# An attention stage with four rooms for probability parts and two for exponentials, and W_out's low parts and the first mixed heads on VectorE

## The chip, the cores and the metric

One core of a Trainium2 chip runs the whole kernel. The time is the device time of one execution in microseconds (us), here always the median of several executions. The engines of the core are named as the profile names them: PE (TensorE, matrix products; PEld its weight loads), DVE (VectorE), ACT (ScalarE), POOL (GpSimd) and SP (SyncE, whose queue issues nearly all transfers; SPq are its issues). They run side by side, each in its own order, and wait for one another through semaphores.

## The reference

One layer of an encoder for 2048 tokens of width 1024. Three groups of heads read the same normalised projection, are gated, and are projected back:

```python
proj = h @ w_in[l]
aq, ak, av, bqkv, ba, bb, mq, z = jnp.split(proj, pts, axis=-1)
...
    def block(qblk):
        sc = jnp.einsum('bkgqd,bksd->bkgqs', qblk, kt).astype(jnp.float32)
        p = jax.nn.softmax(sc, axis=-1).astype(vt.dtype)
        return jnp.einsum('bkgqs,bksd->bkgqd', p, vt)
...
mix = jnp.concatenate([y_a, y_b, y_m], axis=-1) * jax.nn.silu(z)
x = x + rms_norm(mix @ w_out[l], norm_post_w[l])
```

`y_a` is softmax attention with 8 heads over all 2048 tokens, `y_b` a gated delta rule, and `y_m` attention of 4 heads into 256 memory tokens. The change lies in the stage that computes `y_a` and `y_m`, in the preparation of `w_out`, and in the first rows of `mix` that are made ready for `mix @ w_out`.

## The kernel before

Products that need float32 accuracy are made of float16 parts: a value is a high part (its float16 cast) plus a low part (what the cast left over), and a product is three matmuls (high by high, high by low, low by high).

The stages follow each other: projections and the delta rule up to about 1300 us, attention from 1307 to about 2085 us, then the output projection. Attention is cut into 136 blocks: 64 units of 256 queries of one head, two blocks of 128 queries (`qb` 0 and 1) each, and after every fourth of the first 32 units one memory unit, which is one block. So there are 72 units; their index `n` is that of `prefetch`.

A block goes through these steps, one pass of the main loop apart (`lag(1)`, `lag(2)`, up to `LAG` = 5):

- pass i: `score(k)` for k = 0 and 1: six matmuls of 128x512 into a PSUM pair (`sa`; three such pairs exist), and `top(k)`: a maximum over 1024 scores on DVE; after k = 1 two short DVE instructions give the softmax offset (`mx`).
- pass i+1: `expo(k)` on ACT: the exponentials of 1024 scores into a float32 tile `P` (tag `P`), which frees the PSUM pair; then `high` on ACT: `P` is cast into the high half of a float16 tile `hl` (tag `hl`).
- pass i+2, k = 0: `low`: P minus its high part into the low half of `hl`, 768 keys on DVE and the other 1280 (with one of overlap, which keeps the two in order) on POOL; then SP issues a transposing transfer of the whole `hl`, 1 MB, to `PT`.
- from pass i+6: `value`: PE multiplies `PT` with V (`pva`), in slots between the score matmuls.

A `P` room is needed from a block's first exponential to the end of POOL's `low`; an `hl` room from `high` until the transposing transfer has landed. Both tiles take 8 KB in each partition. Before the change there are three rooms of each.

PE, ACT and DVE run in the order in which the code is written in this stage (they are pinned). POOL and SP are not: a scheduler places their instructions, and then they too run in that fixed order.

`prefetch(n)` prepares the output projection during the last 32 units (n from 40): for odd n up to 55 `split_wo` splits one 128x1024 piece of W_out into its parts (`wo`), fetched one unit before into the only `wraw` room (`wor`); for n = 57, 59 and 61 `split_mix` gates, scales and splits the first four heads of `mix` for one block of 128 tokens (`mer` times `mr_r`, into `me`), fetched for even n. It runs at the head of a pass, with `qb` = 0, ahead of the exponentials. With POOL as the engine `split_wo` takes two ACT instructions and one on POOL; `split_mix` one on ACT and three on POOL.

At the end of attention the remaining heads of `mix` for the first two token blocks (`mr`, `mg`) borrow rooms of the tags `P` and `hl`, and PE fills the gaps with output matmuls on the three early `me` blocks (`fillers`).

Of the kernel before, what the change touches and what calls it, by code (L numbers as in the profile page):

```python
# [22 lines left out]
S = 2048  # L23
# [14 lines left out]
def hybrid_layer(ctx: ExitStack, tc: tile.TileContext, t: dict, out, dbg=None):  # L38
# [1102 lines left out]
    class Block:  # L1141
# [46 lines left out]
        def expo(self, k):  # L1188
            if k == 0:
                self.P = p.tile([128, 2, 1024], F32, tag="P", name=f"P{self.nm}", bufs=3)  # L1190
            ps = self.halves[k]
# [40 lines left out]
        def high(self):  # L1232
            hl = self.hl = p.tile([128, 2, S], F16, tag="hl", name=f"hl{self.nm}", bufs=3, align_bytes=512)
            P = self.P.rearrange("p a c -> p (a c)")
            A.copy(hl[:, 0], P)
            n = self.u["n"]
            if n in (2, 3) and len(PT) == n:
                PT.append(late_slot(f"PT{n}", [128, 2, 2, 16, 128], F16))
            self.pt = PT[n % 4][:, self.qb]
# [76 lines left out]

    def split_wo(kc, raw, eng):
        hi, lo = (wo[kc // 4][:, i, kc % 4] for i in range(2))
        sc = wos[:, kc // 2:kc // 2 + 1]
        if eng is G:  # L1320
            A.activation(raw, raw, AF.Copy, scale=sc)
            A.copy(hi, raw)
            G.tensor_tensor(lo, raw, hi, op=ALU.subtract)
        else:
            A.activation(hi, raw, AF.Copy, scale=sc)
            V.scalar_tensor_tensor(lo, raw, sc, hi, op0=ALU.mult, op1=ALU.subtract)

# [16 lines left out]

    def split_mix(fetched, m, eng):
        raw, g, r, n = fetched
        G.tensor_tensor(r, r, g, op=ALU.mult)
        eng.tensor_tensor(raw[:, 0:n], raw[:, 0:n], r[:, 0:n], op=ALU.mult)
        if raw.shape[1] > n:
            eng.tensor_tensor(raw[:, n + 4:], raw[:, n + 4:], r[:, n:], op=ALU.mult)  # L1350
        A.copy(m[:, 0], raw)
        eng.tensor_tensor(m[:, 1], raw, m[:, 0], op=ALU.subtract)
# [4 lines left out]

    early, raws = [], {}

    def prefetch(n):  # L1360
        if n in (40, 48):
            wo.append(slot(f"wo{n}", [128, 2, 4, D], F16))
        k, odd = divmod(n - 40, 2)
        if k < 0:
            return
        if k < 8:
            if odd:
                split_wo(k, raws.pop(k), G)
            else:
                raws[k] = fetch_wo(k, wp, 1)  # L1370
        elif k < 11:
            if odd:
                early.append(wp.tile([128, 2, 4, 128], F16, tag="whl", name=f"me{k - 8}", bufs=4))
                split_mix(raws.pop(k), early[-1], G)
            else:
# [24 lines left out]
    for i in range(len(blocks) + LAG + 1):  # L1400
# [14 lines left out]
        if new and new.qb == 0:  # L1415
            prefetch(new.u["n"])
            if new.u["n"] % 5 < 2 and 5 <= new.u["n"] < 37:
# [6 lines left out]
        if len(blocks) < i <= len(blocks) + 4:  # L1424
            kc = i - len(blocks) + 7
            split_wo(kc, raws.pop(kc), V)
            if kc < 11:
                raws[kc + 1] = fetch_wo(kc + 1, wp, 1)
        for tb in range(2):
            n = i - len(blocks) - 2 * tb - LAG + 4  # L1430
            if n == 1:
                side = p.tile([128, S], F32, tag="hl", name=f"mg{tb}", bufs=3, align_bytes=512)
                raws["mix", tb] = fetch_mix(tb, 4, 16, p.tile([128, S], F32, tag="P", name=f"mr{tb}", bufs=3), side, side[:, 1024:])
            if n == 2:
                mhl.append(slot(f"mhl{tb}", [128, 2, 16, 128], F16))
                split_mix(raws.pop(("mix", tb)), mhl[tb][:, :, 4:, :], V)
        for k in range(2):
# [6 lines left out]
            if k == 0 and lag(2):  # L1444
                lag(2).low()
            if k == 1 and ex:
                ex.high()
            if not new:
                for _ in range(3):
# [20 lines left out]
    with ExitStack() as es:  # L1470
# [42 lines left out]
        for kc in range(4, 16):  # L1513
            if kc > 11:
                split_wo(kc, fetch_wo(kc, p, 2, "x" if kc % 2 else "ot"), V)
            for tb in range(2):
# [56 lines left out]
```

## Time and profile before

| what | us |
|---|---|
| median of 3 runs | 2432.86 (2427.4 to 2435.85) |
| the profiled execution's own time | 2420.37 |
| its span in the profile | 2418.6 |
| PE / DVE / ACT / POOL busy | 2309.8 / 1647.2 / 1300.1 / 747.1 |
| first exponential of attention | 1307.12 |
| first exponential of block 72 (unit 40) | 1701.39 |
| first exponential of block 117 | 1954.69 |
| first exponential of the last block (135) | 2048.15 |

The page of the profile gives the busy time of each engine. Finer answers come from the trace: who waited for whom in a stretch of time, the instructions of one tile, and all instructions of a few microseconds in order of time. A row of the last kind has the start, the duration, the engine, the operation, what it writes and reads, and in brackets how long the engine stood idle ahead of it and what ended that.

### The profile page before, as it was taken

The numbers are of one execution on the slowest core, as the hardware profiler recorded it, in microseconds if no ns is written. First come the engines' busy times: TensorE is split into PE (matmuls) and PEld (weight loads), VectorE is DVE, ScalarE is ACT, GpSimd is POOL, SyncE is SP. The second block draws the span as 40 slices with busy tenths as digits, with TensorE's granted clock in tenths as the row PEclk, the third lists the DMA queues.
The fourth block names the chain that finished last, engine by engine and source line by source line (L and its number), as shares of the span: only waits on it lengthen the run. The fifth ranks groups of instructions, "written<-read, shape, count | busy, mean of one in ns | idle before, by whom it ended". The sixth has DMA issues, their size and how long they took to land.

```text
span 2418.6 us, 42214 instructions
## 1 busy us (share of the span) xinstructions
PE 2309.8 (96%) x15838; PEld 1463.6 (61%) x15846; DVE 1647.2 (68%) x3321; ACT 1300.1 (54%) x2516; POOL 747.1 (31%) x448
## 2 busy tenths in 40 slices
PE   6999999999999999999999999999999999899998
PEld 5888874455554446767764566666666666444443
DVE  7777558999767855555554787778867777355553
ACT  5634436644443145565555788888888788111110
POOL 2146431111311221121122444444555654122110
PEclk9999999999999999999999999999999999999999
DMA  6456555344387576677866999999999999685551
GB/s 227 140 131 152 128 118 171 118 116 126 118 261 234 112 212 207 209 238 222 258 210 193 243 244 241 239 234 247 244 235 235 235 240 219 189 252 189 174 183 53
DMA packets 942125, 471.58 MB, mean 195 GB/s; under 512 B 721952, under 2 KB 889440, under 8 KB 941664
## 3 DMA queue, kind: packets, MB, share of 16 engines
q1 hardware_dynamic: 929472, 425.88, 69.0%
q0 software_dynamic: 12448, 43.00, 5.3%
q8 instruction: 125, 2.05, 0.3%
q14 instruction: 80, 0.66, 0.1%
HBM read 207.59 MB, written 108.10 MB: 131 GB/s over the span
## 4 chain that ended last, share of the span: by engine, by line
PE 60%; DMA 15%; DVE 9%; issue 6%; ACT 4%; POOL 3%; SPq 3%; DVEq 0%; ACTq 0%; POOLq 0%
PE o L51 12%; PE z L51 11%; PE sa L51 8%; PE pva L51 7%; PE q L51 6%; DMA PT<-hla 6%; PE b L51 5%; SPq L51 2%; DMA xx<-bx 2%; PE av L51 2%; POOL hla L51 2%; DMA wor<-in_w_out 2%; DVE y L51 1%; PE tx L51 1%; DMA NI<-nit 1%
## 5 line engine op out<-in xcount | busy, mean ns | idle before, releaser
L51 PEld LDWEIGHTS <-wparts 128*128 128x128 f16 x3072 | 293.5, 98 | 316.7 <-issue 6.2
L51 POOL TENSOR_TENSOR hla<-Pa,hla 128x1281 f16<-128x1281 f32 x128 | 335.7, 2623 | 302.5 <-DVE hla L51 288.7
L51 DVE TENSOR_REDUCE mxa<-sa 128x1 f32<-128x1024 f32 x256 | 313.2, 1224 | 150.4 <-PE sa L51 148.2
L51 PE MATMUL sa<-K,qa 128*128 128x512 f16 x1536 | 374.4, 380 | 32.8 <-ACT Pa L51 30.3
L51 PE MATMUL z<-hT,wparts 128*128 128x512 f16 x1536 | 375.6, 382 | 5.0 <-POOL wparts L51 4.7
L51 PE MATMUL pva<-PT,V 128*128 128x256 f16 x3072 | 376.4, 273 | 0.0
L51 PEld LDWEIGHTS <-V 128*128 128x128 f16 x3072 | 300.6, 98 | 84.9
L51 ACT ACTIVATE Pa<-sa,mxa,misc 128x1024 f32<-128x1024 f32 x256 | 305.6, 1197 | 50.1 <-DVE mxa L51 47.5
L51 PE MATMUL o<-wo,mhl 128*128 128x512 f16 x1416 | 309.4, 382 | 9.3 <-ACT mhl L51 8.0
L51 ACT CAST hla<-Pa 128x2048 f16<-128x2048 f32 x128 | 243.0, 1899 | 72.5 <-DMA PT<-hla 63.4
L51 PE MATMUL b<-hT,wparts 128*128 128x512 f16 x1152 | 257.9, 380 | 0.0
L51 PEld LDWEIGHTS <-mhl 128*128 128x128 f16 x1464 | 143.6, 98 | 184.9 <-ACT mhl L51 8.3
L51 PEld LDWEIGHTS <-qa 128*128 128x128 f16 x1536 | 150.4, 98 | 169.4 <-issue 40.1
L51 PEld LDWEIGHTS <-hT 128*128 128x128 f16 x2304 | 226.0, 99 | 39.9 <-DVE t L51 9.4
L51 PE MATMUL q<-wparts,hT 128*128 128x256 f16 x1920 | 213.6, 275 | 8.8 <-DVE t L51 8.8
L77 POOL DMA_DIRECT2D gate<-zg x64 | 35.5, 554 | 414.9 <-DVE zg L51 282.5
L51 POOL TENSOR_SCALAR wraw<-wraw,wsc 128x1024 f32<-128x1024 f32 (+1 forms) x22 | 76.3, 3468 | 277.9 <-DVE wy L51 277.8
L51 ACT CAST mhl<-mr 128x2048 f16<-128x2048 f32 (+1 forms) x16 | 29.1, 1818 | 224.4 <-PE o L51 173.5
L51 DVE SCALAR_TENSOR_TENSOR y<-xb,convw,y 128x512 f32<-128x512 f32 x192 | 147.8, 782 | 2.0
L51 DVE SCALAR_TENSOR_TENSOR hla<-Pa,hla 128x768 f16<-128x768 f32 x128 | 128.5, 1004 | 2.3 <-ACT hla L51 2.3
L51 POOL TENSOR_TENSOR mg<-mg 128x1536 f32<-128x1536 f32 (+1 forms) x16 | 54.3, 3394 | 242.8 <-DMA mg<-r 174.2
L51 DVE TENSOR_TENSOR mhl<-mr,mhl 128x2048 f16<-128x2048 f32 (+1 forms) x16 | 46.4, 2901 | 87.8 <-ACT mhl L51 87.8
(359 smaller groups left out, 3201.3 us busy)
## 6 DMA issues: line engine op xcount, KB each, us to landing
xx<-bx SPq DMA_DIRECT2D x64, 512.0 KB
wraw<-in_w_in POOLq DMA_DIRECT2D x42, 512.0 KB, 5.3
wor<-in_w_out SPq DMA_DIRECT2D x32, 512.0 KB
gate<-zg POOLq DMA_DIRECT2D x64, 256.0 KB, 3.7
NI<-nit SPq DMA_DIRECT2D x32, 512.0 KB
mr<-mix SPq DMA_DIRECT2D x13, 1024.0 KB
mg<-r SPq DMA_DIRECT2D x13, 768.0 KB
x<-in_x SPq DMA_DIRECT2D x16, 512.0 KB
```

The lines of the kernel that those rows point to most:

```text
L51: ins = f(*args, **kw)
L77: nc.gpsimd.dma_start(to, of)
```

## The change

The tag `hl` gets four rooms, the tag `P` two; together they take what three and three took. The high part of a W_out piece is one ACT instruction that scales and casts, for all 16 pieces; for the pieces that `prefetch` splits, the low part is one DVE instruction, put off to the next pass, after that pass's second maximum. The three early `split_mix` run on DVE, with the cast on ACT as before, and at `qb` = 1 in place of 0. `prefetch` is called after `high`, not at the head of a pass.

```diff
-                self.P = p.tile([128, 2, 1024], F32, tag="P", name=f"P{self.nm}", bufs=3)
+                self.P = p.tile([128, 2, 1024], F32, tag="P", name=f"P{self.nm}", bufs=2)
...
-            hl = self.hl = p.tile([128, 2, S], F16, tag="hl", name=f"hl{self.nm}", bufs=3, align_bytes=512)
+            hl = self.hl = p.tile([128, 2, S], F16, tag="hl", name=f"hl{self.nm}", bufs=4, align_bytes=512)
...
-    def split_wo(kc, raw, eng):
+    def split_wo(kc, raw, later=None):
         hi, lo = (wo[kc // 4][:, i, kc % 4] for i in range(2))
         sc = wos[:, kc // 2:kc // 2 + 1]
-        if eng is G:
-            A.activation(raw, raw, AF.Copy, scale=sc)
-            A.copy(hi, raw)
-            G.tensor_tensor(lo, raw, hi, op=ALU.subtract)
+        def low():
+            V.scalar_tensor_tensor(lo, raw, sc, hi, op0=ALU.mult, op1=ALU.subtract)
+
+        A.activation(hi, raw, AF.Copy, scale=sc)
+        if later is None:
+            low()
         else:
-            A.activation(hi, raw, AF.Copy, scale=sc)
-            V.scalar_tensor_tensor(lo, raw, sc, hi, op0=ALU.mult, op1=ALU.subtract)
+            later.append(low)
...
-    def split_mix(fetched, m, eng):
+    def split_mix(fetched, m, eng, first=G):
         raw, g, r, n = fetched
-        G.tensor_tensor(r, r, g, op=ALU.mult)
+        first.tensor_tensor(r, r, g, op=ALU.mult)
...
-        if k < 0:
+        if k < 0 or qb != (8 <= k < 11 and odd):
             return
         if k < 8:
             if odd:
-                split_wo(k, raws.pop(k), G)
+                split_wo(k, raws.pop(k), lows)
...
-                split_mix(raws.pop(k), early[-1], G)
+                split_mix(raws.pop(k), early[-1], V, V)
...
         if new and new.qb == 0:
-            prefetch(new.u["n"])
...
-                side = p.tile([128, S], F32, tag="hl", name=f"mg{tb}", bufs=3, align_bytes=512)
-                raws["mix", tb] = fetch_mix(tb, 4, 16, p.tile([128, S], F32, tag="P", name=f"mr{tb}", bufs=3), side, side[:, 1024:])
+                side = p.tile([128, S], F32, tag="hl", name=f"mg{tb}", bufs=4, align_bytes=512)
+                raws["mix", tb] = fetch_mix(tb, 4, 16, p.tile([128, S], F32, tag="P", name=f"mr{tb}", bufs=2), side, side[:, 1024:])
...
             if k == 1 and ex:
+                while lows:
+                    lows.pop()()
                 ex.high()
+                if new:
+                    prefetch(new.u["n"], new.qb)
```

On POOL, at units 39 to 42, the order before is this (`hla` and `hlm` are the low parts of blocks of attention and of memory units, `wo` a low part of W_out):

```order
L51 TENSOR_TENSOR hlm_0_18857<-Pm_0_18812,hlm_0_18857 128x1281
L51 TENSOR_TENSOR wo_18807<-wor_18808,wo_18807 128x1024
L51 TENSOR_TENSOR hla_0_0_18912<-Pa_0_0_18874,hla_0_0_18912 128x1281
L51 TENSOR_TENSOR hla_0_1_18976<-Pa_0_1_18937,hla_0_1_18976 128x1281
L51 TENSOR_TENSOR hla_256_0_19032<-Pa_256_0_18995,hla_256_0_19032 128x1281
L51 TENSOR_TENSOR hla_256_1_19089<-Pa_256_1_19051,hla_256_1_19089 128x1281
L51 TENSOR_TENSOR wo_18807<-wor_19047,wo_18807 128x1024
```

And in the changed kernel:

```order
L51 TENSOR_TENSOR hlm_0_18854<-Pm_0_18809,hlm_0_18854 128x1281
L51 TENSOR_TENSOR hla_0_0_18912<-Pa_0_0_18874,hla_0_0_18912 128x1281
L51 TENSOR_TENSOR hla_0_1_18973<-Pa_0_1_18934,hla_0_1_18973 128x1281
L51 TENSOR_TENSOR hla_256_0_19031<-Pa_256_0_18993,hla_256_0_19031 128x1281
L51 TENSOR_TENSOR hla_256_1_19086<-Pa_256_1_19048,hla_256_1_19086 128x1281
```

POOL has nothing but the low parts of blocks from there to the end of attention: eight `wo` rows and nine rows of the early mix have left it.

On DVE, in the pass where unit 41's second block is scored, the changed kernel has this (`mxa` are maxima and offsets, `hla` DVE's share of a low part, `moa` a copy of a finished output):

```order
L51 TENSOR_REDUCE mxa_256_1_19002<-sa_256_1_0_18995 128x1
L51 SCALAR_TENSOR_TENSOR hla_0_1_18973<-Pa_0_1_18934,hla_0_1_18973 128x768
L51 TENSOR_REDUCE mxa_256_1_19002<-sa_256_1_1_19020 128x1
L51 TENSOR_SCALAR mxa_256_1_19002<-mxa_256_1_19002,misc 128x1
L51 TENSOR_SCALAR mxa_256_1_19002<-mxa_256_1_19002 128x1
L51 SCALAR_TENSOR_TENSOR wo_18856<-wor_18857,wos,wo_18856 128x1024
L51 COPY moa_1536_18948<-pva_1536_0_18949 128x256
L51 TENSOR_REDUCE mxa_512_0_19057<-sa_512_0_0_19050 128x1
```

The `wo` row is new; the other rows stand there before too, in the same order. At unit 57 the early mix comes at the same point of a pass:

```order
L51 TENSOR_SCALAR mxa_256_1_20769<-mxa_256_1_20769 128x1
L51 TENSOR_TENSOR mr_r_20630<-mr_r_20630,mer_20629 128x512
L51 TENSOR_TENSOR mer_20629<-mer_20629,mr_r_20630 128x512
L51 TENSOR_TENSOR me_20801<-mer_20629,me_20801 128x512
L51 TENSOR_REDUCE mxa_512_0_20829<-sa_512_0_0_20822 128x1
```

The three `TENSOR_TENSOR` rows are new on DVE; between the second and the third lies ACT's cast of `mer`.

On SP, where attention ends, the rows between the last two transposing transfers were these before:

```order
L1246 DMA_TRANSPOSE PT_15091<-hla_1792_0_22340 128x32x128
L51 DMA wor_22409<-in_w_out 128x1024
L51 DMA mr_22466<-mix 128x12x128
L51 DMA mg_22465<-gate 128x4x128
L51 DMA mg_22465<-gate 128x4x128
L51 DMA mg_22465<-r 128x1024
L51 DMA mr_22573<-mix 128x12x128
L51 DMA mg_22572<-gate 128x4x128
L1246 DMA_TRANSPOSE PT_15091<-hla_1792_1_22383 128x32x128
L51 DMA wor_22463<-in_w_out 128x1024
```

And in the changed kernel:

```order
L1246 DMA_TRANSPOSE PT_15091<-hla_1792_0_22332 128x32x128
L51 DMA wor_22401<-in_w_out 128x1024
L51 DMA mr_22458<-mix 128x12x128
L51 DMA mg_22457<-gate 128x4x128
L51 DMA mg_22457<-gate 128x4x128
L51 DMA mg_22457<-r 128x1024
L51 DMA mg_22564<-gate 128x4x128
L51 DMA mg_22564<-gate 128x4x128
L1246 DMA_TRANSPOSE PT_15091<-hla_1792_1_22375 128x32x128
L51 DMA wor_22455<-in_w_out 128x1024
```

The second block's `mr` (768 KB) has moved behind the last transposing transfer, and its second gate part (256 KB) ahead of it.

More of the change, by code (lines that the diff above doesn't have):

```diff
@@ L1356, in out_mm, with prefetch @@
             T.matmul(ps[:, hf, :], m[:, m_, k, :], w[:, w_, kc % 4, hf * 512:(hf + 1) * 512], start=(kc == 0 and i == 0), stop=(kc == 15 and i == 2))
-    early, raws = [], {}
-    def prefetch(n):
-        if n in (40, 48):
+    early, raws, lows = [], {}, []
+    def prefetch(n, qb):
+        if n in (40, 48) and qb == 0:
             wo.append(slot(f"wo{n}", [128, 2, 4, D], F16))
         k, odd = divmod(n - 40, 2)
-        if k < 0:
+        if k < 0 or qb != (8 <= k < 11 and odd):
             return
@@ L1425, in hybrid_layer @@
             kc = i - len(blocks) + 7
-            split_wo(kc, raws.pop(kc), V)
+            split_wo(kc, raws.pop(kc))
             if kc < 11:
@@ L1514, in hybrid_layer @@
             if kc > 11:
-                split_wo(kc, fetch_wo(kc, p, 2, "x" if kc % 2 else "ot"), V)
+                split_wo(kc, fetch_wo(kc, p, 2, "x" if kc % 2 else "ot"))
             for tb in range(2):
```

## The prediction

> **What bounds the kernel now.** I read the page first, then who waited for whom in the attention stage by stretches of time, then single passes in order of time, and last the tail of that stage.
>
> ```profile
> span 2418.6 us, 42214 instructions
> PE 2309.8 (96%) x15838; PEld 1463.6 (61%) x15846; DVE 1647.2 (68%) x3321; ACT 1300.1 (54%) x2516; POOL 747.1 (31%) x448
> PE sa L51 <- ACT Pa L51: 5.4, 3, 4.0
> PE sa L51 <- ACT Pa L51: 9.4, 9, 2.5
> PE sa L51 <- ACT Pa L51: 15.2, 13, 2.1
> PE o L51 <- ACT mhl L51: 8.0, 1, 8.0
> ```
>
> PE is busy for 96% of the span, so only its waits can be won. The three `sa` rows are the stretches 1300 to 1400, 1400 to 1700 and 1700 to 1950 us: score matmuls waited 30.0 us there for exponentials to free a PSUM pair. From 1950 to 2050 they waited 0.4 us. The last row is one wait at the end of attention. This is all that the change can touch: nothing before attention moves on any engine.
>
> Why are exponentials late? Up to 1700 us because ACT's cast, just ahead of the next exponentials, waits for an `hl` room, that is, for a transposing transfer to land:
>
> ```profile
> ACT hla L51 <- DMA PT<-hla: 30.5, 22, 3.7
> 1513.19 5.34 SPq L1246 DMA_TRANSPOSE PT<-hlm  x1
> 1563.52 4.14 SPq L1246 DMA_TRANSPOSE PT<-hlm  x1
> 2022.66 4.13 SPq L1246 DMA_TRANSPOSE PT<-hla  x1
> ```
>
> The first row covers 1400 to 1700 us. The two `hlm` rows are one memory block and the next, nine blocks later: (1563.52 - 1513.19) / 9 = 5.59 us a block. SP's rows follow one another there with hardly a gap. A transposing issue that finds the queue free takes 4.13 us (last row), so SP with its other issues is the limit in that stretch, at 5.59 against PE's 5.21 (below). After 1950 us it keeps up.
>
> A pass without disturbance, the stretch in which PE loses nothing:
>
> ```profile
> 2003.06 0.95 DVE L51 SCALAR_TENSOR_TENSOR hla<-Pa,hla 128x768 f16<-128x768 f32 x1
> 2004.09 2.62 POOL L51 TENSOR_TENSOR hla<-Pa,hla 128x1281 f16<-128x1281 f32 x1 [2.59 <-DVE hla L51]
> 2006.09 0.15 DVE L51 TENSOR_SCALAR mxa<-mxa 128x1 f32<-128x1 f32 x1
> 2006.36 1.21 ACT L51 ACTIVATE Pa<-sa,mxa,misc 128x1024 f32<-128x1024 f32 x1 [0.80 <-DVE mxa L51]
> 2007.13 1.22 DVE L51 TENSOR_REDUCE mxa<-sa 128x1 f32<-128x1024 f32 x1 [0.88 <-PE sa L51]
> 2008.24 1.46 PE L51 MATMUL sa<-K,qa 128*128 128x512 f16 x6
> 2008.27 0.95 DVE L51 SCALAR_TENSOR_TENSOR hla<-Pa,hla 128x768 f16<-128x768 f32 x1
> 2013.48 0.95 DVE L51 SCALAR_TENSOR_TENSOR hla<-Pa,hla 128x768 f16<-128x768 f32 x1
> ```
>
> The period is 2008.27 - 2003.06 = 5.21 us, set by PE. POOL's low part of block 125 (2004.09) ends at 2006.71. The exponential at 2006.36 is that of block 127.
>
> **The change part by part.**
>
> *Two rooms for P.* Block 127's first exponential must now wait for POOL's low part of block 125; before, for that of 124, done 5 us earlier. What a POOL to ACT release takes, and how soon PE follows an exponential:
>
> ```profile
> 269.18 4.88 POOL L51 TENSOR_SCALAR wraw<-wraw,wsc 128x1024 f32<-128x1024 f32 x1
> 274.09 1.04 ACT L51 CAST wparts<-wraw 128x1024 f16<-128x1024 f32 x1 [1.51 <-POOL wraw L51]
> 1522.48 1.20 ACT L51 ACTIVATE Pa<-sa,mxa,misc 128x1024 f32<-128x1024 f32 x1
> 1523.82 1.46 PE L51 MATMUL sa<-K,qa 128*128 128x512 f16 x6 [0.24 <-ACT Pa L51]
> ```
>
> POOL ends at 274.06, ACT starts at 274.09: 0.03 us. PE follows 1523.82 - 1522.48 = 1.34 us after an exponential's start. So in every undisturbed pass the exponential starts at 2006.74, 0.38 us late. PE would be held only past 2008.24 - 1.34 = 2006.90, that is, by a delay over 0.54 us. The new wait is in every pass and costs nothing by itself; behind it on ACT stand the second exponential and the cast, which would end at 2006.74 + 2 x 1.2 + 1.9 = 2011.0, ahead of its reader, DVE's low part at 2013.48. But a loop now closes over two blocks: low part to exponential 3.65 + 0.03, to PE 1.34, from there to the low part two blocks on 2013.48 - 2008.24 = 5.24; together 10.26 of 10.42 us. Spare 0.16 us. Delays that three rooms swallowed now reach PE.
>
> At the eight memory blocks ACT has no slack to hide it:
>
> ```profile
> 1548.07 0.56 ACT L51 ACTIVATE Pm<-sm,mxm,undo 128x256 f32<-128x256 f32 x1
> 1554.38 1.20 ACT L51 ACTIVATE Pa<-sa,mxa,misc 128x1024 f32<-128x1024 f32 x1
> ```
>
> A memory block holds ACT for 6.31 us, more than the period, so the 0.38 us goes on top: 8 x 0.38 = **+3.0** (at least 0, where SP is the limit anyway; at most 1.0 each, 8).
>
> *Four rooms for hl.* Where SP is the limit, a room more cannot raise its rate. It lets ACT and PE run one block further ahead of SP, once, and SP pays it back after 1950 us where it has slack: one block at SP's rate, **-5.6** (between 0 and the 14.8 us of the first two `sa` rows). Both together for the first 72 blocks: -2.6.
>
> *The work that prefetch moves* (units 40 to 63, blocks 72 to 117):
>
> ```profile
> 1701.39 1.20 ACT L51 ACTIVATE Pa<-sa,mxa,misc 128x1024 f32<-128x1024 f32 x1
> 1954.69 1.20 ACT L51 ACTIVATE Pa<-sa,mxa,misc 128x1024 f32<-128x1024 f32 x1
> L51 ACT ACTIVATE wor<-wor,wos 128x1024 f32<-128x1024 f32 x8 | 9.2, 1144 | 0.0
> L51 ACT CAST wo<-wor x8: 1044/1045/1047, 1707.2 to 1864.8; 128x1024 f16<-128x1024 f32 x8
> L51 POOL TENSOR_TENSOR wo<-wor,wo x8: 2124/2136/2852, 1708.3 to 1865.9; 128x1024 f16<-128x1024 f32 x8
> 1754.32 1.46 PE L51 MATMUL sa<-K,qa 128*128 128x512 f16 x6 [1.84 <-ACT Pa L51]
> ```
>
> These are the first exponentials of blocks 72 and 117: 253.30 us for 45 blocks, where 45 x 5.21 = 234.45 would do; 18.85 us are lost. Two ACT instructions (1.14 and 1.05 us) stand ahead of a pass's exponentials eight times, as in the last row, where PE waited 1.84 us; and POOL's 2.14 us ahead of a low part makes that transfer late, so the cast two or three blocks on waits again. The scaling pass is dropped, the other ACT instruction goes behind the cast, where a pass has 5.21 - 4.31 = 0.9 us idle (ACT's own work is 2 x 1.2 + 1.9); its 1.15 us makes the exponential 0.25 us late, less than the 0.38 that it waits anyway. POOL loses 8 x 2.14 us and the nine rows of the early mix. Of the 18.85 I take 0.8 as staying (small transposes on PE): **-18.0**.
>
> What comes instead stands on DVE, between 2006.24 (the end of the row 2006.09) and the next maximum at 2007.13, ahead of the next low part, and so inside the tight loop:
>
> ```profile
> L51 DVE SCALAR_TENSOR_TENSOR wo<-wor,wos,wo x4: 1274/1282/1285, 2054.5 to 2086.0; 128x1024 f16<-128x1024 f32 x4
> 2045.88 2.63 POOL L51 TENSOR_TENSOR hla<-Pa,hla 128x1281 f16<-128x1281 f32 x1 [2.59 <-DVE hla L51]
> 2047.99 1.32 DVE L51 SCALAR_TENSOR_TENSOR hla<-Pa,hla 128x768 f16<-128x768 f32 x1
> 2087.69 1.27 DVE L51 TENSOR_TENSOR mr<-mr,mg 128x512 f32<-128x512 f32 x2
> L51 ACT CAST me<-mer 128x512 f16<-128x512 f32 x3 | 1.8, 612 | 0.0
> ```
>
> The same low part of W_out takes DVE 1.28 us later in the program. It would begin while POOL still works. The second and third rows show what that does: DVE's usual 0.95 us became 1.32 where it overlapped POOL's last 0.52 us (2047.99 to 2048.51), 0.37 more. So 1.65 us, then the copy of a finished output (0.41), in a place with 0.89 us: some 1.0 us late (starts overlap ends by about 0.1 each). The next low part, POOL's part and the exponential behind it are late by 0.38 + 1.0, and PE stands 0.84 us: 8 x 0.84 = **+6.7** (0.24 each if the copy and the overlap cost nothing, 1.3 each if nothing overlaps).
>
> The Trainium skill (SBUF — State Buffer, section "Who interferes with whom") says that a DVE instruction with two SBUF inputs contends with a GpSimd instruction that reads SBUF, and that the later one is blocked for the whole rest of the earlier. The row agrees but for 0.15 us (0.37 against 0.52). By the rule each of the eleven moved pieces would lose the full 0.47 us from 2006.24 to 2006.71 and not 0.37, and the sum would be 1.1 us worse.
>
> The early mix, three times: two multiplications (1.27 + 0.37), ACT's cast (0.61), the last subtraction (0.64 by the same row). ACT is in order, so the next exponential stands behind the cast: 2006.24 + 1.64 + 0.06 + 0.61 = 2008.55, 2.19 late, PE 1.65; the subtraction makes the next maximum late for another 0.25. 3 x 1.9 = **+5.7** (between 0.8 and 3.3 each).
>
> In the last 16 blocks nothing is added but the 0.38, hidden; I put **+0.5** for the small DVE rows of every eighth block.
>
> *The tail.* PE's 8.0 us hang on a W_out transfer behind the last transposing issue:
>
> ```profile
> GB/s 227 140 131 152 128 118 171 118 116 126 118 261 234 112 212 207 209 238 222 258 210 193 243 244 241 239 234 247 244 235 235 235 240 219 189 252 189 174 183 53
> ...
> 2064.47 8.16 SPq L1246 DMA_TRANSPOSE PT<-hla  x1
> 2073.07 0.35 SPq L51 DMA_DIRECT2D wor<-in_w_out  x1
> 2076.89 1.15 ACT L51 ACTIVATE wo<-wor,wos 128x1024 f16<-128x1024 f32 x1 [14.75 <-DMA wor<-in_w_out]
> ```
>
> That issue took 8.16 us and not 4.13 because 3.3 MB of loads went ahead; by the order it is now 2.8 MB. (8.16 - 4.13) x 0.5/3.3 is 0.6 us, at the rate of the attention stage (some 240 GB/s in the first row, slices 22 to 33 of 40) 2.1. I take **-2.0** (0 to -4).
>
> Sum: -2.6 - 18.0 + 6.7 + 5.7 + 0.5 - 2.0 = **-9.7** us. Against the profiled execution's own 2420.37 that is 2410.7; that execution lies 12.5 us below the median of the runs shown, so against the median 2432.86 it is **2423.2**.
>
> **The rivals.**
>
> 1. *Slower: the loop over two P rooms becomes the bound.* Its spare is 0.16 us of 10.42. If low part, POOL and exponential together take longer than the rows say, by a later release or because DVE and POOL now meet at other moments, each of 64 turns pays the excess. It turns the change slower from 9.7 / 64 = 0.15 us beyond the spare, 0.31 in all. At 0.45 in all it is 64 x 0.29 - 9.7 = +8.9: 2441.8. For it: the spare is smaller than the 0.37 of one overlap. Against it: the steady rows repeat to 0.02 us, and POOL's 2.62 us does not move. Chance 0.11.
> 2. *No difference: DVE gives back what POOL and ACT win.* With 1.3 us for each W_out piece and 3.3 for each mix, and SP's rate so firm that the fourth room wins nothing: 3.0 - 18.0 + 10.4 + 9.9 + 0.5 - 2.0 = +3.8; with half of these excesses and of the 5.6, about -3: 2430. For it: SP without gaps. Chance 0.22.
> 3. *The fourth room takes all waits away*, memory blocks included, and the DVE rows take their low ends: 30.0 us less 3.0, 1.9 and 2.4, about -22: 2411. For it: DVE is only 68% busy. Against it: SP's 5.59 us. Chance 0.12.
>
> **How the numbers follow.** The forecast (-5 to -16) has 0.55. A measurement of this kernel tells 0.3%, 7.3 us, from no change. Four fifths of the forecast lie beyond that, with rival 3 that makes 0.56 for faster; the other fifth and rival 2 make 0.33 for the same; rival 1 is 0.11 for slower. The range goes from just under rival 3 (2409) to 2436, past rival 2 and its +3.8, short of rival 1.
>
> **What would show it.** Right: ACT's waits for landings mostly gone; in their place POOL ending 0.03 us ahead of the first exponential in most passes, with no PE wait there; POOL without gaps of two kinds from 1700 us on; blocks 72 to 117 in some 247 us; short PE waits once in four blocks where a W_out row stands on DVE, and three longer ones at the mixes. Wrong: a period above 5.21 us in the last 16 blocks (rival 1), SP still without gaps and ACT still waiting for landings after 1700 us (rival 2), or PE waits under 8 us in all of attention (rival 3).

## The result, and the profile after

| | before | after |
|---|---|---|
| median, us | 2432.85 (2427.4 to 2435.85, 4 runs) | 2410.99 (2407.9 to 2416.47, 4 runs) |
| ratio, with its 95% interval | | 0.9918 (0.9897 to 0.994) |
| span of the profiled execution | 2418.6 | 2405.8 |

The change made the kernel faster by 21.9 us; the interval of the ratio lies wholly below 1. The time lies inside the predicted range, near its lower end; the forecast was 9.7 us. The direction was right and the size was not, so the question is where the other 12 us came from.

The waits of PE after, in the same five stretches as before (total in us, times, longest; 1950 to 2040 us has none):

```profile
PE sa L51 <- ACT Pa L51: 2.4, 2, 1.5
PE sa L51 <- ACT Pm L51: 1.1, 1, 1.1
...
PE sa L51 <- ACT Pm L51: 7.4, 7, 1.1
...
PE sa L51 <- ACT Pa L51: 7.6, 14, 1.5
...
PE o L51 <- ACT mhl L51: 3.4, 1, 3.4
PE o L51 <- DVE mhl L51: 2.2, 2, 1.2
```

Waits for `Pa` up to 1700 us fell from 14.8 to 2.4 us, and 8.5 us for `Pm` (memory blocks, 1.1 each) took part of their place. From 1700 to 1950 us 15.2 became 7.6; the wait at the end 8.0 became 3.4, while the waits behind DVE just after it rose from 1.4 to 2.2.

ACT's waits from 1400 to 1700 us, whose first row before was the wait for landings (30.5 us, 22 times):

```profile
ACT Pa L51 <- POOL hla L51: 31.5, 37, 1.0
ACT Pm L51 <- PE sa L51: 8.4, 7, 1.2
ACT Pa L51 <- POOL hlm L51: 3.3, 6, 0.5
```

No `hl` cast waits for a landing any more; instead the first exponential waits for POOL, as the prediction said. An undisturbed pass shows how closely:

```profile
1996.40 2.62 POOL L51 TENSOR_TENSOR hla<-Pa,hla 128x1281 f16<-128x1281 f32 x1 [2.58 <-DVE hla L51]
1999.06 1.21 ACT L51 ACTIVATE Pa<-sa,mxa,misc 128x1024 f32<-128x1024 f32 x1 [0.80 <-POOL hla L51]
2000.55 1.46 PE L51 MATMUL sa<-K,qa 128*128 128x512 f16 x6
```

POOL ends at 1999.02, the exponential starts 0.04 us later, and PE follows without a wait in brackets. The period is still 5.21 us (the next low part on POOL starts at 2001.61).

The stage times, cut at the first exponentials (columns: window, its length, then the busy time of each engine with its instructions, the granted clock, the DMA share, GB/s; the last window ends 292.8 us ahead of the end of the span). Before, then after:

```profile
1307.12:1701.39 394.27, 378.82 (x2623) 256.44 (x2621) 308.24 (x473) 328.66 (x459) 187.80 (x74) 1.00 1.09 237
1701.39:1954.69 253.30, 238.04 (x1634) 159.47 (x1633) 187.65 (x275) 213.73 (x245) 148.85 (x63) 1.00 1.08 239
1954.69:2037.73 83.04, 82.61 (x573) 55.81 (x571) 63.48 (x96) 70.08 (x81) 41.62 (x16) 1.00 1.06 226
2037.73:2125.82 88.09, 78.76 (x457) 44.90 (x456) 35.60 (x39) 28.28 (x30) 17.96 (x8) 0.94 0.71 193
```

```profile
1313.70:1701.95 388.25, 377.33 (x2623) 256.16 (x2621) 306.18 (x473) 332.11 (x460) 187.90 (x74) 1.00 1.10 240
1701.95:1946.46 244.51, 236.91 (x1626) 158.70 (x1625) 198.55 (x290) 206.89 (x237) 118.08 (x45) 1.00 1.14 244
1946.46:2030.43 83.97, 83.97 (x582) 56.70 (x581) 63.86 (x96) 70.06 (x81) 41.99 (x16) 1.00 1.10 238
2030.43:2113.00 82.57, 77.00 (x455) 44.57 (x453) 33.97 (x39) 28.44 (x29) 18.03 (x7) 0.98 0.73 204
```

The differences are -6.0, -8.8, +0.9 and -5.5, together -19.4 us. The part ahead of attention is unchanged work and took 6.6 us more in this execution (the first exponential at 1313.70, not 1307.12); in the other profiles of this study, a second one of the kernel before among them, it came at 1311 to 1320. So spans of single executions say little here, and the experiments are read by stage times, cut in the same way: "0-72" is from the first exponential of block 0 to that of block 72.

### The profile page after: what moved, and what is told of

The parts are those of the page before. It is cut to its first block, busy times and chain, and to the rows that moved or that the text cites. A ratio compares the mean times of both kernels' runs of the same rounds, so it can differ in the third digit from the quotient of the medians.

```text
span 2405.8 us, 42213 instructions
## 1 busy us (share of the span) xinstructions
PE 2308.4 (96%) x15846; PEld 1463.4 (61%) x15846; DVE 1652.5 (69%) x3338; ACT 1297.4 (54%) x2508; POOL 717.7 (30%) x431
## 5 line engine op out<-in xcount | busy, mean ns | idle before, releaser
L51 PE MATMUL sa<-K,qa 128*128 128x512 f16 x1536 | 373.0, 379 | 20.7 <-ACT Pa L51 10.0
L51 DVE SCALAR_TENSOR_TENSOR hla<-Pa,hla 128x768 f16<-128x768 f32 x128 | 121.7, 951 | 0.0
```

What stands on the lines that cost most here:

```text
L51: ins = f(*args, **kw)
```

## The experiments

All stage times in one table (us). Each ratio is to runs of the kernel before that were made beside the kernel in the row (their medians are 2432.06 to 2433.47), so it is not the quotient of two medians of this table; the stage times come from one profile of each kernel.

| kernel | median | ratio to before | 0-72 | 72-117 | 117-133 |
|---|---|---|---|---|---|
| before | 2432.85 | | 394.27 | 253.30 | 83.04 |
| before, profiled again | 2433.01 (1 run) | | 397.40 | 255.65 | 83.04 |
| after | 2410.99 | 0.9918 (0.9897 to 0.994) | 388.25 | 244.51 | 83.97 |
| rooms alone | 2423.91 | 0.9972 (0.9957 to 0.9986) | 388.25 | 254.89 | 83.58 |
| prefetch alone | 2426.76 | 0.9975 (0.9961 to 0.9989) | 393.18 | 247.99 | 85.48 |
| two P, three hl | 2424.79 | 0.9977 (0.9963 to 0.9991) | 393.99 | 247.37 | 83.96 |
| 1024 keys on DVE | 2409.2 | 0.9913 (0.9892 to 0.9934) | 386.48 | 242.64 | 83.74 |
| loads and stores on POOL's queue | 2432.37 | 0.9999 (0.9982 to 1.0015) | 408.92 | 244.60 | 83.96 |
| more issues on SP | 2433.2 | 1.0001 (0.9988 to 1.0014) | 406.35 | 244.93 | 84.50 |
| W_out's low parts on POOL | 2422.73 | 0.9962 (0.9948 to 0.9976) | 388.29 | 254.01 | 83.97 |
| early mix spread | 2413.93 | 0.993 (0.9907 to 0.9953) | 388.28 | 248.75 | 83.96 |
| P of half width, three rooms | 2418.61 | 0.9947 (0.9927 to 0.9967) | 390.41 | 245.61 | 85.00 |
| early mix spread, own room | 2417.47 | 0.9926 (0.9905 to 0.9946) | 388.21 | 245.11 | 85.22 |
| the same, 1024 keys | 2408.81 | 0.9897 (0.9874 to 0.992) | 386.57 | 242.62 | 85.72 |

### The two halves of the change, and the split between its rooms

The first kernel is the one before with the new room counts alone; the second has the moved work alone; the third has the change without its fourth `hl` room. (No run has three `P` and four `hl` rooms of full width.)

The edits in short:

```diff
 rooms alone (on the kernel before)
-P bufs=3, hl bufs=3
+P bufs=2, hl bufs=4
 prefetch alone (on the changed kernel)
-P bufs=2, hl bufs=4
+P bufs=3, hl bufs=3
 two P, three hl (on the changed kernel)
-hl bufs=4
+hl bufs=3
```

> The kernel before with only the rooms changed (two for P, four for hl); the prefetch stays at the head of a pass and on POOL. My theory (the two parts of the change work in different stretches): blocks 0 to 72 take what the changed kernel takes (388 us, before 394), blocks 72 to 117 keep most of their loss (250 us or more, before 253, changed 244.5), since the eight W_out pieces on POOL now stand inside the tight loop of two P rooms. In all 6 to 9 us faster than before. Rival (the fourth hl room does nearly all of it): blocks 72 to 117 drop to about 245 us as well, and the whole is some 18 us faster.

> The changed kernel with three rooms for P and three for hl, so only the moved prefetch. My theory: blocks 0 to 72 as before (394 us, ACT waiting for landings again), blocks 72 to 117 within 2 us of the changed kernel (243 to 246 us). In all 8 to 12 us faster than before. Rival (rooms do nearly all of it): blocks 72 to 117 stay above 250 us.

> The changed kernel with three hl rooms and still two for P. Theory A, which the delay of SP in the changed kernel's trace suggests (its transposing issues start up to 6 us after POOL is done, which three hl rooms do not allow): ACT waits for landings come back on top of the wait for POOL, blocks 0 to 72 take 394 us or more, blocks 72 to 117 248 or more; 8 to 12 us slower than the changed kernel. Theory B, that of the prediction (SP is at its limit anyway, a room is a credit of one block, once): 5 to 6 us slower, all of it in one place.

The rooms alone give the whole gain of blocks 0 to 72 (388.25, the same as after to 0.01 us) and nothing in 72 to 117, where POOL still has W_out's parts. The moved work alone gives most of 72 to 117 (-5.3) and nothing ahead. The third kernel divides the rooms: with two `P` rooms and three `hl` rooms blocks 0 to 72 take 393.99, so giving up a `P` room cost nothing measurable against either profile of before, and the fourth `hl` room is worth 393.99 - 388.25 = 5.7 us there and 247.37 - 244.51 = 2.9 us more in blocks 72 to 117. The two stage differences of the third kernel come from one profile each, and with three `hl` rooms such times vary by some 3 us (see the last experiment). Its whole time is 13.8 us above the changed kernel, more than either theory had; 2.8 us of the difference between the two profiles lie behind block 133. The prefetch alone missed its expectation: 247.99 us and not 243 to 246, and by its ratio 6 us gained and not 8 to 12.

The parts do not add up: rooms alone +1.6 and prefetch alone -5.3 make -3.7 in 72 to 117, together they make -8.8. The next experiment shows one reason.

### W_out's low parts back on POOL

```diff
...
-            later.append(low)
+            A.activation(raw, raw, AF.Copy, scale=sc)
+            A.copy(hi, raw)
+            G.tensor_tensor(lo, raw, hi, op=ALU.subtract)
```

> The changed kernel with the eight early W_out pieces split as before (scaling pass and cast on ACT, low part on POOL), but at the new place behind the block's cast. Theory 1 (POOL's 2.1 us ahead of a low part is what cost PE before, and with two P rooms the exponential two blocks on waits for it): blocks 72 to 117 take 249 to 254 us in place of 244.51, with ACT waiting 1.5 us and more for POOL eight times. Theory 2 (the place at the head of the pass was the cost, and DVE's 1.28 us is no cheaper than POOL): within 1.5 us of 244.51. All other stages unchanged within 0.5 us.

Blocks 72 to 117 took 254.01 us, 9.5 more, as theory 1 had it, but of PE's waits at the pieces POOL accounts for the smaller part. The edit brings back ACT's scaling pass too, so ACT again has two instructions ahead of a pass's exponentials. The rows of one piece (the second last is the exponential two blocks on from the first):

```profile
1760.06 1.14 ACT L51 ACTIVATE wor<-wor,wos 128x1024 f32<-128x1024 f32 x1
1761.23 1.05 ACT L51 CAST wo<-wor 128x1024 f16<-128x1024 f32 x1
1762.18 1.20 ACT L51 ACTIVATE Pa<-sa,mxa,misc 128x1024 f32<-128x1024 f32 x1
1762.36 2.13 POOL L51 TENSOR_TENSOR wo<-wor,wo 128x1024 f16<-128x1024 f32 x1 [1.44 <-ACT wo L51]
1763.53 1.46 PE L51 MATMUL sa<-K,qa 128*128 128x512 f16 x6 [0.82 <-ACT Pa L51]
...
1768.03 1.20 ACT L51 ACTIVATE Pa<-sa,mxa,misc 128x1024 f32<-128x1024 f32 x1 [1.44 <-POOL hla L51]
1769.38 1.45 PE L51 MATMUL sa<-K,qa 128*128 128x512 f16 x6 [0.48 <-ACT Pa L51]
```

The first wait of PE stands behind the two ACT instructions: 0.61 to 0.93 us, 6.8 us for the eight pieces. The second comes from POOL's 2.1 us through the two `P` rooms: 0.48 us, 3.9 for the eight. The rooms alone have the same two waits at each piece (0.92 to 0.96 and 0.37 to 0.49 us), so the gain of blocks 0 to 72 does not go on there. What ACT's two instructions or POOL's one would cost without the other was not run.

### Is SP the limit in blocks 0 to 72?

Three kernels bear on it. One takes ordinary loads and stores off SP, one adds 136 small issues to it, and one frees the `P` rooms.

```diff
 loads and stores on POOL's queue
-        dma(q, qT_d[h, :, :, q0:q0 + 2 * QW])
+        wdma(q, qT_d[h, :, :, q0:q0 + 2 * QW])
...
 more issues on SP, behind each transposing issue
+            dma(more_d[blocks.index(self)], at["misc"][0:4, 0:128])
...
 P of half width
-self.P = p.tile([128, 2, 1024], F32, tag="P", name=f"P{self.nm}", bufs=2)
+self.P = p.tile([128, 2, 1024], mybir.dt.bfloat16, tag="P", name=f"P{self.nm}", bufs=3)
...
```

> The changed kernel, with the loads of q and of the memory queries and the stores of finished outputs issued by POOL's queue in place of SP's: some ten issues of 0.55 us for every nine blocks leave SP, whose rows stand without gaps up to block 117 in the changed kernel too. Theory A (SP's issuing sets the pace there, and the fourth hl room was a one-time credit): blocks 0 to 72 take 380 to 384 us in place of 388.25, and blocks 72 to 117 241 to 242 in place of 244.51. Theory B (in the changed kernel the pace is set by the P rooms at the memory blocks, where alone PE waits; SP is late but within its rooms): blocks 0 to 72 within 1.5 us of 388.25, SP with gaps, blocks 72 to 117 within 1.5 of 244.51. Both: POOL's own issues (0.6 us) may make a low part late and cost up to 0.5 us each, at most some 10 us in all; this would show as waits of ACT for POOL above 1 us.

> The changed kernel with one more issue of 2 KB on SP after each transposing transfer (136 in all, some 0.5 us of SP each by the rows of small stores). Theory A (SP sets the pace up to block 117): the load shows in full, about 0.5 us a block: blocks 0 to 72 +30 to +36 us, blocks 72 to 117 +20 to +23. Theory B (SP is late but within its rooms): the first two or three us of it are swallowed by the lag that four rooms allow, and then SP binds: blocks 0 to 72 +10 to +28, blocks 72 to 117 +10 to +20. In both blocks 117 to 133 take less than 3 us more, since a transposing issue takes 4.1 to 4.3 us there of a period of 5.21.

> The changed kernel with P as bfloat16, which halves its rooms, so that three of them fit beside four hl rooms (this alters the values: the low part of P loses most of its bits; the late mix rows borrow hl rooms instead, so only the time up to block 133 is compared). In the changed kernel every nine blocks with a memory block among them take 48.46 us, where nine blocks without one take 47.00. Theory A (the 1.46 us are the price of two P rooms at the memory block): groups of 47.2 to 47.9 us, blocks 0 to 72 in 377 to 384 us in place of 388.25, no waits of PE for Pm. Theory B (SP's issuing, 48.5 us for nine blocks, is as tight): groups of 48.2 to 49, blocks 0 to 72 in 386 to 391, with ACT waiting for landings again. Theory C (ACT's 6.3 us at a memory block cost PE 1.1 us by themselves): groups of 48.0 to 48.4 without waits for landings. If DVE's or POOL's rows come out shorter with 16-bit input, that part is named apart.

**The third is the clean one**, since the long rows keep their durations with P of half width (exponentials 1.20 us, casts 1.90, DVE's low part 0.95, POOL's 2.61 and not 2.62). It changes the values and the rows of the mixed heads at the end, so only its time up to block 133 is compared. POOL's low parts from 1400 to 1700 us (total and mean of one, then the idle time before them), in the changed kernel:

```profile
L51 POOL TENSOR_TENSOR hla<-Pa,hla 128x1281 f16<-128x1281 f32 x50 | 131.2, 2624 | 133.8 <-DVE hla L51 133.8
```

and with P of half width:

```profile
L51 POOL TENSOR_TENSOR hla<-Pa,hla 128x1281 f16<-128x1281 bf16 x49 | 128.1, 2614 | 140.9 <-DVE hla L51 140.9
```

The first exponentials of blocks 27, 36 and 45 of the changed kernel:

```profile
1459.61 1.20 ACT L51 ACTIVATE Pa<-sa,mxa,misc 128x1024 f32<-128x1024 f32 x1
...
1508.08 1.20 ACT L51 ACTIVATE Pa<-sa,mxa,misc 128x1024 f32<-128x1024 f32 x1
...
1556.55 1.20 ACT L51 ACTIVATE Pa<-sa,mxa,misc 128x1024 f32<-128x1024 f32 x1
```

Nine blocks with a memory block among them take 48.47 us here, and 48.46 to 48.47 in every such group from block 9 to 72; before they took 47.6 to 50.0. Nine blocks without one take 47.00 at the end of attention. So steady a number hardly comes from transfers; it is the memory block, behind which PE waits 1.1 us each time. The other 0.4 us are work of PE. With three `P` rooms ACT's waits from 1400 to 1700 us are these:

```profile
ACT hla L51 <- DMA PT<-hla: 34.6, 24, 3.2
ACT Pa L51 <- DVE mxa L51: 7.9, 18, 0.8
ACT hla L51 <- DMA PT<-hlm: 4.6, 5, 1.5
```

PE has no wait for `Pm` any more in that stretch, and yet blocks 0 to 72 take 390.41 us, 2.2 more, because ACT waits for landings again. This is theory B: at 390.41 x 9 / 72 = 48.8 us for nine blocks SP is just as tight as the two `P` rooms, though single groups vary more than theory B said (47.80 to 50.42 us from block 9 to 72, where 48.2 to 49 were expected). The price of the `P` rooms at the memory blocks is paid out of time in which the landings would have been late.

The added issues agree where they took place. The scheduler did not place them where the code has them: of the 136, 52 stood ahead of attention, 44 in blocks 0 to 18, 40 in blocks 18 to 72 and none behind, so the expectation for the later stretches was not tested. In blocks 18 to 72 the other issues of SP rose from 30.9 to 43.5 us (62 and 102 of them), and the stretch from 290.80 to 303.85 us: 12.6 us of SP, 13.05 us of time. ACT's waits for landings were back (29.5 us, 21 times, from 1400 to 1700 us). In blocks 0 to 18 as much of SP (23.0 us of other issues in place of 10.4) cost only 5.05 us, since SP could still fall behind: its transposing issue started 3.0 us after POOL's low part at block 16 of the changed kernel, and 8.9 us here. So SP has a lag to spend, once, and no reserve behind it.

The relief failed, and for a reason of its own: at 408.92 us blocks 0 to 72 lie 20.7 us above the changed kernel, outside what either theory had. SP lost 40 of those 62 issues (30.9 to 9.0 us), but the transposing issues grew from a mean of 4.61 to one of 5.20 us, 32 us for 54 of them; one alone took 14.5 us, and without it the mean is 5.03. So the same loads from another queue did not shorten SP's work here. On POOL, two issues ahead of the low part in front of each memory block made the `Pm` wait 2.1 us in place of 1.1. It does not tell A from B. The shortest transposing issues of 1 MB take 3.9 to 4.0 us (3.94 in blocks 18 to 72 of the changed kernel, 3.98 in blocks 117 to 133). The Trainium skill (DMA: Bandwidth & Descriptors, section "Latency and other measured facts") states an effective 261 GB/s for a transposing transfer with a non-contiguous middle dimension, from which 4.0 us for 1 MB is an estimate; the trace agrees, but no run here shows whether this transfer is of that form.

### A low part with more keys on DVE, and the early mix spread over passes

```diff
 1024 keys
-    DVE_KEYS = 768
+    DVE_KEYS = 1024
...
 early mix spread: product now, cast and subtraction one pass later each
-                split_mix(raws.pop(k), early[-1], V, V)
+                split_mix_late(raws.pop(k), early[-1])
...
+        V.tensor_tensor(r, raw, r, op=ALU.mult)
+        def cast():
+            A.copy(m[:, 0], r)
+            lows.append(lambda: V.tensor_tensor(m[:, 1], r, m[:, 0], op=ALU.subtract))
+        casts.append(cast)
...
 own room: the product goes to the unused half of me's room
-                early.append(wp.tile([128, 2, 4, 128], F16, tag="whl", name=f"me{k - 8}", bufs=4))
+                room = wp.tile([128, 4, 4, 128], F16, tag="whl", name=f"me{k - 8}", bufs=4)
```

> The changed kernel with DVE taking 1024 of the 2048 keys of a low part and not 768. POOL's part gets shorter by 256 keys (about 0.5 us of 2.62), DVE's longer by about 0.28. Theory (the loop over two P rooms costs time wherever a pass is disturbed): the first exponential of a pass moves from 0.38 us late to about 0.15 late, undisturbed passes keep 5.21 us, and the passes at memory blocks and behind W_out pieces win some 0.2 us each: 2 to 5 us faster than the changed kernel. Rival (the loop costs nothing anywhere, DVE's own queue does): 0 to 5 us slower, since DVE has 0.28 us more in each pass.

> The changed kernel with the early mix spread over three passes: the two products on DVE at the same place, ACT's cast one pass later behind that pass's cast, the subtraction another pass later (the product stays in mr_r's room). Theory 1 (each early mix costs PE 1.9 us because the exponentials stand behind ACT's cast, which waits for DVE): blocks 72 to 117 take 239.5 to 241.5 us in place of 244.51, and ACT's wait of 6.2 us for mer goes. Theory 2 (SP without gaps sets the pace of this stretch): 243.5 or more, with waits for landings in place of those for DVE. All other stages unchanged within 0.5 us.

> The changed kernel with the early mix spread over three passes as in the late mix before, but the product in a place of its own (the unused half of me's room), so that the next fetch of mr_r waits for nothing new and keeps its place in SP's order. Theory 1 (the exponentials stand behind ACT's cast, which waits 2.1 us for DVE): 1.4 us less for each of three, as the first of them showed in the run before; blocks 72 to 117 in 239.5 to 241.5 us in place of 244.51, no wait of DVE for mr_r. Theory 2 (SP sets the pace there): 243.5 or more, with ACT waiting for landings. Whole time 2407 us against the 2411 of the changed kernel by theory 1.

> The same with 1024 keys of a low part on DVE in place of 768: POOL's part ends some 0.2 us earlier in each pass. By the two runs that had one of these alone: blocks 0 to 72 in 386.5 us, blocks 72 to 117 in 238 to 240 us by theory 1; 241 or more by theory 2 or if DVE, with 0.32 us more in each pass, becomes late where W_out's low parts and the mix stand on it. Whole time 2404 to 2407 us by theory 1.

1024 keys shorten nine blocks from 48.47 to 48.25 us and blocks 72 to 117 by 1.9; in the whole time, where 2 to 5 us were expected, this can't be told from the change (0.9913 and 0.9918, intervals overlapping). The first spread mix lost 4.2 us. The row shows why:

```profile
1921.27 0.69 DVE L51 TENSOR_TENSOR mr_r<-mr_r,mer 128x512 f32<-128x512 f32 x1 [5.66 <-DMA mr_r<-r]
```

The product stayed in `mr_r` for two passes more, so the fetch of the next `mr_r` was placed two transposing issues later, and DVE, in order, stood 5.66 us for it. With a room of its own that wait is gone, and the gain still does not come (245.11; theory 2):

```profile
ACT Pa L51 <- POOL hla L51: 23.4, 27, 1.7
ACT hla L51 <- DMA PT<-hla: 12.5, 11, 3.5
```

ACT's 6.2 us of waiting for `mer` turned into 12.5 us of waiting for landings, which were 0.2 us after the change (all from 1700 to 1950 us). The three longest, 3.0, 3.5 and 2.3 us, stand at the three mixes: there SP is as late as the cast was, and taking the cast away wins nothing. With 1024 keys as well the median is 2408.81, the lowest of the study and above the 2404 to 2407 of theory 1, but its interval overlaps that of the changed kernel: no version here is shown to beat it.

### The kernel before, profiled again

> The kernel before, unchanged, profiled once more, to see which of the stage times repeat. If the tail of attention was shortened by the change, its last transposing issue takes some 8.2 us again and PE waits some 8 us for the cast of the mixed heads, and from the first exponential of block 133 to the output matmul behind the last wait it takes 88 us. If the first profile was an unlucky one there, the issue takes 6.4 to 7.4 us as in the kernels with the old prefetch or the old rooms, the wait is 4 to 5 us and the stretch 84 to 86. Blocks 0 to 72, 72 to 117 and 117 to 133 take 394.3, 253.3 and 83.0 us again, within 1.5 us.

The tail repeats: the last transposing issue takes 8.24 us, PE's wait 7.9, and from the first exponential of block 133 to the output matmul behind the wait it takes 46.5 us, after 46.6 in the first profile (2084.31 - 2037.73), and 41.6 in the changed kernel. (The 88 us of the expectation belong to a later end, that of the last window above.) The stages with three `hl` rooms do not repeat within the 1.5 us expected (+3.1 and +2.3 us), while the five kernels with two `P`, four `hl` rooms and 768 keys whose traffic is untouched take 388.21 to 388.29 us for blocks 0 to 72. That waiting for landings is what varies from one execution to another fits this, and is not shown by itself. Against the mean of both profiles of before the change gains 7.6 and 10.0 us in the first two stretches.

## Why the prediction was right in sign and short in size

| step | predicted | measured |
|---|---|---|
| two P rooms, blocks 0 to 72 | +3.0 | none found (-0.3 to -3.4, two P and three hl rooms against before) |
| four hl rooms, blocks 0 to 72 | -5.6 | -5.7 |
| both, blocks 0 to 72 | -2.6 | -6.0 |
| W_out's low parts on DVE | +6.7 | +2.4 (PE's waits) |
| early mix | +5.7 | +5.2 (PE's waits) |
| blocks 72 to 117 in all | -5.6 | -8.8 |
| last 16 blocks | +0.5 | +0.9 |
| tail, to the output matmul | -2.0 | -4.9 |

**The P loop held.** POOL's end 0.04 us ahead of the exponential, no PE wait behind it and the period of 5.21 us are as worked out. Rival 1 fell: a spare of 0.16 us in 10.42 was enough.

**The P rooms at memory blocks.** The step put 8 x 0.38 us on top of SP's limit. PE's own waits for `Pm` are larger, 8.5 us, at the upper bound; but they came in place of waits for landings, not on top of them. Its lower bound, "at least 0, where SP is the limit anyway", was the answer: of two limits that are about equal only one is paid.

**The fourth hl room.** -5.6 was right for 0 to 72, within the 3 us by which such stages vary. That SP is the limit was right too, though 5.59 us a block came from a single group that was slow: from block 18 (1408.23 us) to block 72 (1701.39) the mean is 293.16 / 54 = 5.43. The step failed in that it counted the credit once: 2.9 us more came in blocks 72 to 117. SP's rows show why. In the changed kernel its transposing issue starts up to 5.4 us after POOL's low part in blocks 0 to 72 (block 43), only 2.3 us after it at block 72, up to 6.1 at block 103, and at most 0.6 from block 125 to 132; before, it was never more than 4.2 and 2.8 us in these two stretches. The lag was spent, partly paid back, and spent again.

**W_out on DVE.** The row's duration was right: 1.61 us against the 1.65 predicted. PE's waits were not:

```profile
L51 DVE SCALAR_TENSOR_TENSOR wo<-wor,wos,wo x8: 1605/1610/1624, 1717.1 to 1866.6; 128x1024 f16<-128x1024 f32 x8
1725.10 1.46 PE L51 MATMUL sa<-K,qa 128*128 128x512 f16 x6 [0.59 <-ACT Pa L51]
1746.36 1.46 PE L51 MATMUL sa<-K,qa 128*128 128x512 f16 x6 [0.26 <-ACT Pa L51]
...
1874.26 1.46 PE L51 MATMUL sa<-K,qa 128*128 128x512 f16 x6 [0.26 <-ACT Pa L51]
```

One wait of 0.59 and seven of 0.26 us make 2.4. The copy of a finished output, 0.42 us, stands behind the W_out row only the first time; the other seven times it comes a pass later. The prediction read the order at one place and charged its copy eight times: 7 x (0.59 - 0.26) = 2.3 of the 4.3 us between 6.7 and 2.4. The other 2.0 are the unit price, 0.84 against 0.59 with the copy. The price without one had been named as the lower bound, 0.24. The overlap was sized well: the row began 0.53 us before POOL's low part ended and took 0.33 us more than its 1.28, where 0.37 was expected.

**The early mix.** Periods of 7.11, 7.00 and 7.12 us (blocks 106, 110, 114) against 5.21, and PE's waits:

```profile
1889.05 0.69 DVE L51 TENSOR_TENSOR mer<-mer,mr_r 128x512 f32<-128x512 f32 x1
1889.78 0.62 ACT L51 CAST me<-mer 128x512 f16<-128x512 f32 x1 [2.11 <-DVE mer L51]
1890.30 1.20 ACT L51 ACTIVATE Pa<-sa,mxa,misc 128x1024 f32<-128x1024 f32 x1
1891.64 1.46 PE L51 MATMUL sa<-K,qa 128*128 128x512 f16 x6 [1.48 <-ACT Pa L51]
1897.25 1.46 PE L51 MATMUL sa<-K,qa 128*128 128x512 f16 x6 [0.24 <-ACT Pa L51]
```

The exponential stands behind the cast, and the cast behind DVE: 1.48 and 0.24 us, where 1.65 and 0.25 were expected. These 7.6 us of waits in 72 to 117 leave 16.4 us for what was removed, against 18.0. They are what PE waited and not what another version would win: without the cast's wait SP's landings came as late.

**The tail.** In the changed kernel (before: 8.16 us for the issue, and the piece of W_out scaled at 2076.89):

```profile
2054.89 7.19 SPq L1246 DMA_TRANSPOSE PT<-hla  x1
2066.79 1.15 ACT L51 ACTIVATE wo<-wor,wos 128x1024 f16<-128x1024 f32 x1 [12.80 <-DMA wor<-in_w_out]
```

From block 133's first exponential to that scaling it takes 2066.79 - 2030.43 = 36.4 us, where it took 2076.89 - 2037.73 = 39.2: 2.8 us, within the bounds of 0 to 4. The other 2.1 of the 4.9 were not in the sum at all. DVE's and POOL's products for the mixed heads before (each row of DVE is two products):

```profile
2079.28 3.43 DVE L51 TENSOR_TENSOR mr<-mr,mg 128x512 f32<-128x512 f32 x2
2079.72 2.44 POOL L51 TENSOR_TENSOR mg<-mg 128x1024 f32<-128x1024 f32 x1 [10.77 <-DMA mg<-r]
```

and after:

```profile
2069.18 1.29 DVE L51 TENSOR_TENSOR mr<-mr,mg 128x512 f32<-128x512 f32 x2
2073.15 2.86 POOL L51 TENSOR_TENSOR mg<-mg 128x1024 f32<-128x1024 f32 x1 [11.82 <-DMA mg<-r]
```

Before, POOL's product of the second token block began inside DVE's two short products, and the second of these ended only 0.55 us after POOL (2082.16), so that the pair took 3.43 us in place of 1.29 (a product alone takes 0.69). In the changed kernel the second block's loads land later, and POOL starts 2.7 us after the pair has ended. The Trainium skill (SBUF — State Buffer, section "Who interferes with whom") states that a DVE instruction with two SBUF inputs contends with a GpSimd instruction that reads SBUF, and that the later of the two is blocked for the whole rest of the earlier; here the trace agrees.

How much of the tail's gain lasts is open, for POOL's product now meets DVE's next row. With two `P` and three `hl` rooms, whose end is written the same:

```profile
2081.16 2.34 POOL L51 TENSOR_TENSOR mg<-mg 128x1024 f32<-128x1024 f32 x1 [10.56 <-DMA mg<-r]
2081.32 3.80 DVE L51 TENSOR_TENSOR mhl<-mr,mhl 128x1536 f16<-128x1536 f32 x1 [1.58 <-ACT mhl L51]
2085.17 1.46 PE L51 MATMUL o<-wo,mhl 128*128 128x512 f16 x3 [3.23 <-DVE mhl L51]
```

In the changed kernel DVE's row began 1.1 us ahead of POOL's and took 1.76 us; POOL's took 2.86 in place of 2.34, and PE waited 1.19. With the rooms alone, W_out's low parts on POOL, and the two spread mixes with 768 keys, it went as in the third kernel (3.46 to 3.93 us for DVE's row). From block 133 to the end of the span these five take 378.1 to 379.2 us, the changed kernel 375.4, before 380.9 and 380.3. So some 3 us of the gain behind block 133 may be the luck of one execution, and the -2.0 of the prediction is about what the five show.

With the measured stages in place of the predicted ones the sum is -9.7 - 3.4 (blocks 0 to 72) - 3.2 (72 to 117) + 0.4 - 2.9 (tail) = -18.8, against -19.4 for the stages, whose last reaches 0.6 us further than the tail's row. This adds up by construction; it tells where the sum was off and is no second proof of the causes. The forecast's own band, -5 to -16 us with a chance of 0.55, was missed. The range held because it had been drawn out to take in rival 3, which had 0.12, so that part was luck. The time came out where rival 3 put it, with half of its mechanism: the waits for landings went and W_out's rows took their low end, but the memory blocks' waits stayed (8.5 us of PE), and SP has no reserve behind its lag.

## What to carry to other kernels

Where two limits of about the same height act on one loop, only one of them is paid: price the pair by the later one, not by the sum, and test by relieving each alone. A cost read at one place of the order holds for that place; count the neighbours at every repetition before multiplying. When an experiment puts work back, list every instruction that comes back with it, on every engine. And short DVE rows late in a chain are worth a look for a POOL instruction beside them: which of the two starts first can decide microseconds.

## What was not expected of the hardware

A transposing issue of 1 MB occupies SP for 3.9 us at its shortest and 4.6 on average beside loads (blocks 18 to 72 of the changed kernel), and 5.2 us on average when 40 of the 62 other issues came from another queue; its landing follows 2.0 us after the end of the row (median). The stage's time with three `hl` rooms varied by 3.1 us between two executions of one kernel; with four it came out within 0.1 us in five kernels.
